# Rotary queries and keys of a hybrid layer: one product of 512 columns in place of two of 256

## The chip, the cores and the metric

The program runs on one core of a Trainium2 chip, in one launch. The metric is the device time of an execution in microseconds (us), the median of several runs. The core's engines are TensorE (PE in the rows, with its weight loads as PEld), VectorE (DVE), ScalarE (ACT), GpSimd (POOL) and SyncE (SP, which issues the DMAs here). Sums of products land in PSUM, a small memory that DVE and ACT read out ("evacuate"); everything else on the chip lies in SBUF.

## The reference, cut to what matters

Two layers over 256 tokens of width 2048. The even layer projects the normed input by one wide matrix and cuts the result up; two of the pieces, `rq` and `rk` (1024 columns each, eight heads of 128), are turned by the rotary angles and feed a retention.

```python
h = rms_norm(x, norm_g) @ w_in                       # 256 x 2048 @ 2048 x 7704
rq, rk, rv, rz, nq, kc, vc, ks, vs, kw, vw, ng, nz = split_cols(h, EVEN_SPLITS)
o = retention_chunkwise(rotary(heads(rq, 8), pos), rotary(heads(rk, 8), pos), heads(rv, 8))
...
def rotary(t, pos):
    t1, t2 = tf[..., :64], tf[..., 64:]
    return concatenate([t1 * cos - t2 * sin, t2 * cos + t1 * sin], axis=-1)
```

All is in float32. The kernel gets there by writing each factor of a projection as a high part in a shorter format (fp32r) and the rest: x = xh + xl, w = wh + wl, and the sum xh·wh + xh·wl + xl·wh. So each 128x128 block of weights costs three products.

## The kernel before

The program is a long row of projections. Each one streams its weights from HBM in pieces of 512 KB (128 partitions x 1024 numbers, tile `raw`, lines 100 to 103), ACT copies a piece to its high part (`wh`, L109), DVE subtracts to get the low part (`wl`, L110), and PE takes the products (`project`, L114). Five buffers of each of the three tiles let the loads run ahead. `prep` (L90) has a high priority in the list scheduler, which writes down a fixed order for every engine before the program runs; each engine then works through its own list in that order and waits at the head of it.

Most projections have the input as the stationary factor and 512 columns of weights as the moving one (L145 to L147; 512 columns of output, tokens on partitions). The four projections for the rotary queries and keys are flipped (`flip=True`, called at L680): 128 columns of the weights are stationary and the 256 tokens move, so that the output comes out turned, a head's 128 numbers on partitions and the tokens along a row. These are lines L139 to L141, each on 256 columns. A flipped projection is 512 columns of weights, four heads, in two PSUM tiles (`mm`, three buffers in all) with two heads in each.

When a tile is full, `evac_rotary` (L633) reads it: ACT copies the two halves of the partitions crosswise into `rot` (L640, L641), DVE multiplies the tile by the cosines into `T` (L642), and POOL multiplies `rot` by the sines and adds it (L643, L644). The cosines and sines are first multiplied by the tokens' norms (`rrow`, made by PE and copied by ACT at L235; POOL, L630 and L631, in the tile `pb`).

Between the chunks of a projection, pieces of other work are called (`extra=take(...)`). In the rotary stage these are the eight heads of the selected and windowed attention, `nsa_piece` (L604). A head is: six score products (L550 to L552, three of 512 columns and three of 256) into the PSUM tile `sc`, of which there is one buffer; four steps on DVE that add the mask, write `p` and take the row maximum (L560, with a short read of the maximum behind each); the exponentials on ACT (L567); a scaling on DVE (L574); six transposes on PE (L579); and the split of these by ACT and DVE (L459, L460). Before the first heads, DVE and ACT also write a table `pst` from the compressed attention's probabilities (`pch`, `pcl`; L538, copies of 32 partitions).

```python
        sc = ps.tile([128, 1024], F32, name="sc", tag="sc")
...
            project(ew[4 + 3 * hf + i], 512, lhs, evac_rotary(T), extra=take((1,3)), flip=True)
```

Of the kernel before, what the change touches and what calls it, by code (L numbers as in the profile page):

```python
# [13 lines left out]
F32 = mybir.dt.float32  # L14
# [8 lines left out]
S = 256  # L23
# [11 lines left out]
MMB = 3  # L35
# [6 lines left out]
           (0, 512), (1024, 1536), (2048, 2560), (512, 1024), (1536, 2048), (2560, 3072),  # L42
           (6680, 7192), (7192, 7704), (3072, 3584), (3584, 4096)]
EV_NARROW = (6656, 6680, 4096, 4608)
# [15 lines left out]
def hybrid_kernel(ctx: ExitStack, tc: tile.TileContext, a: dict, out: bass.AP):  # L60
# [53 lines left out]
    def project(src, n, lhs, evac, korder=None, lazy=None, extra=None, cut=None,  # L114
                flip=False):

        nch = src.shape[0]
        acc = [ps.tile([128, 512], F32, name=f"mm{t}", tag="mm", bufs=MMB) for t in range(2)]  # L120
        order = korder or list(range(nch))
        for i, c in enumerate(order):
            if lazy:
                lazy(c)
            parts = prep(src[c], n, cut=(lambda k: cut(c, k)) if cut and i < 3 else None)
            xh, xl = lhs[c]
            for hf in range(2):
                wh, wl = parts[hf]
                for t in range(2):
                    for j in range(2):  # L130
                        for k in range(2):
                            kk = 2 * hf + k
                            first = i == 0 and kk == 0
                            last = i == nch - 1 and kk == 3
                            if flip:
                                cs = slice((2 * t + j) * 128, (2 * t + j) * 128 + 128)
                                o = acc[t][:, j * S:j * S + S]
                                kw = dict(skip_group_check=True)
                                nc.tensor.matmul(o, wh[:, k, cs], xh[:, kk, :], start=first and j == 0, stop=False, **kw)  # L139
                                nc.tensor.matmul(o, wl[:, k, cs], xh[:, kk, :], start=False, stop=False, **kw)  # L140
                                nc.tensor.matmul(o, wh[:, k, cs], xl[:, kk, :], start=False, stop=last, **kw)  # L141
                            elif j == 0:
                                ts = slice(t * 128, t * 128 + 128)
                                o = acc[t][:, :n]
                                nc.tensor.matmul(o, xh[:, kk, ts], wh[:, k, :n], start=first, stop=False)  # L145
                                nc.tensor.matmul(o, xh[:, kk, ts], wl[:, k, :n], start=False, stop=False)  # L146
                                nc.tensor.matmul(o, xl[:, kk, ts], wh[:, k, :n], start=False, stop=last)  # L147
                    if i == nch - 1 and hf == 1:
                        with tc.high_priority(offset=HPO):
                            evac(t, acc[t])  # L150
            for f in (extra or {}).get(i, ()):
                f()
# [28 lines left out]

    def norm_block(b, gain, first=False):

        xh = xtp.tile([128, 4, S], F32R, name="xh", tag="xh")
        xl = xtp.tile([128, 4, S], F32R, name="xl", tag="xl")
# [8 lines left out]
        return xh, xl  # L194
# [51 lines left out]
    def project_both(srcs, accs, evacs):  # L246

        nch = srcs[0].shape[0]
        for c in range(nch):
            for q in range(2):  # L250
# [10 lines left out]
                xh, xl = lhs[c]  # L261
# [371 lines left out]
    def evac_rotary(T):  # L633
        rot = hp.tile([128, 4, S], F32, name="rot", tag="h")

        def f(b, p):
            hs = slice(2 * b, 2 * b + 2)
            pv = p.rearrange("p (h s) -> p h s", h=2)
            cb, sb = (x.unsqueeze(1).to_broadcast([128, 2, S]) for x in (cosR, sinR))
            nc.scalar.copy(rot[0:64, hs, :], pv[64:128])  # L640
            nc.scalar.copy(rot[64:128, hs, :], pv[0:64])  # L641
            nc.vector.tensor_tensor(T[:, hs, :], pv, cb, op=ALU.mult)  # L642
            nc.gpsimd.tensor_tensor(rot[:, hs, :], rot[:, hs, :], sb, op=ALU.mult)  # L643
            nc.gpsimd.tensor_add(T[:, hs, :], T[:, hs, :], rot[:, hs, :])  # L644
        return f
# [29 lines left out]
    for hf in range(2):  # L675
        qk = []
        for i in range(2):
            T = hp.tile([128, 4, S], F32, name=f"rT{i}_{hf}", tag="h")
            qk.append(T)
            project(ew[4 + 3 * hf + i], 512, lhs, evac_rotary(T), extra=take((1,3)), flip=True)  # L680
        v = htile(f"rv{hf}")
        project(ew[6 + 3 * hf], 512, lhs, evac_to(v), extra=take((1,3)))
# [8 lines left out]
    def mix_block(src):  # L691

        xh = xtp.tile([128, 4, S], F32R, name="xh", tag="xh")
        xl = xtp.tile([128, 4, S], F32R, name="xl", tag="xl")
# [5 lines left out]
        return xh, xl  # L700

    def gated(src, dst, r, extra):
# [3 lines left out]
        xh = xtp.tile([128, 4, S], F32R, name="xh", tag="xh")  # L706
        xl = xtp.tile([128, 4, S], F32R, name="xl", tag="xl")
# [11 lines left out]
        return (xh, xl), turn  # L719
# [6 lines left out]
    for i in range(2):  # L726
        block, turn = gated(ew[10 + i], no[i], rstd[0], first(turn, take(range(4))))
        mix.append(block)
    for i in range(2):
# [5 lines left out]
        project(ew[12 + i], 512, lhs, evac_z, extra=first(turn, take(range(4))))  # L735
# [17 lines left out]
    def turned_block(n):  # L753

        xh = xtp.tile([128, 4, S], F32R, name="xh", tag="xh")
        xl = xtp.tile([128, 4, S], F32R, name="xl", tag="xl")
# [9 lines left out]
        nxt.append((xh, xl))  # L766
# [294 lines left out]
```

## Time and profile before

| | |
|---|---|
| median of 3 runs | 939.23 us (939.16 to 939.35) |
| the profiled execution, device time | 939.11 us |
| its span (first to last instruction) | 937.3 us |
| PE busy | 930.5 us, 99% of the span |
| PEld, DVE, ACT, POOL busy | 798.7, 642.3, 507.5, 71.1 us |
| read from HBM | 170.5 MB, 184 GB/s over the span |
| the rotary stage, with the eight attention heads in it | about 133 to 275 us of the span |

A busy time is the union of an engine's instructions; matmuls overlap in the record (a matmul is shown until its results are out), so a step of PE is read from one start to the next, not from the duration. The granted clock is the share of PE's full clock (2.4 GHz) that it was given; 0.5 is 1.2 GHz. A number in brackets after a row of the timeline is the idle time of the engine before it, and what ended it.

### The profile page before, as it was taken

The page shows a single profiled execution, that of the slowest core. Times are in us where ns is not written, and L with a number is a line of the kernel's source. Part 1 is how long each engine was busy: PE and PEld are TensorE (multiplying, and loading weights), DVE is VectorE, ACT ScalarE, POOL GpSimd, SP SyncE. Part 2 cuts the span into 40 slices and gives each one's busy share as a digit, 9 for nine tenths or more (in the row PEclk, how much of TensorE's full clock was granted, in tenths as well). Part 3 has the DMA queues.
Part 4 walks back from the last instruction along what each step waited for, and adds up shares of the span by engine and source line. Part 5 has one row for each costly group of instructions (what it writes and reads, how often), then busy time and mean ns, then how long its engine had stood idle before and what let it go on. Part 6 is the DMA issues. An engine that isn't in the chain of part 4 may idle for free.

```text
span 937.3 us, 13151 instructions
## 1 busy us (share of the span) xinstructions
PE 930.5 (99%) x4949; PEld 798.7 (85%) x4949; DVE 642.3 (69%) x947; ACT 507.5 (54%) x762; POOL 71.1 (8%) x72
## 2 busy tenths in 40 slices
PE   8999999999999999999999999999999999999998
PEld 7889989989998888888888888888888888888886
DVE  7687657875654564654464499999999998546552
ACT  7566656655544544544465353556665444797341
POOL 0111100320220100000000000000000002200000
PEclk9999999999999999999999999999999999999999
DMA  9967754354446555555555555555555656434461
GB/s 332 348 204 220 249 189 149 120 176 156 152 164 207 161 170 182 185 195 181 196 185 168 192 180 180 190 190 190 185 186 185 202 197 189 148 116 157 149 226 53
DMA packets 52512, 173.48 MB, mean 185 GB/s; under 512 B 5728, under 2 KB 10720, under 8 KB 52320
## 3 DMA queue, kind: packets, MB, share of 16 engines
q1 hardware_dynamic: 52304, 172.63, 55.8%
q8 instruction: 39, 0.64, 0.3%
q14 instruction: 25, 0.20, 0.1%
q10 hardware_dynamic: 144, 0.01, 0.0%
HBM read 170.52 MB, written 2.10 MB: 184 GB/s over the span
## 4 chain that ended last, share of the span: by engine, by line
PE 97%; DMA 1%; DVE 1%; ACT 0%; issue 0%; SPq 0%; DVEq 0%
PE mm L145 25%; PE mm L147 25%; PE mm L146 25%; PE mm L139 3%; PE mm L141 3%; PE mm L140 3%; PE tr L315 3%; DMA raw<-in_ew 1%; PE dpo L931 1%; PE dsc L911 1%; PE cmph L377 1%; PE tr L579 1%; PE both L273 1%; PE both L274 0%; PE both L272 0%; PE mm L274 0%
## 5 line engine op out<-in xcount | busy, mean ns | idle before, releaser
L110 DVE TENSOR_TENSOR wl<-raw,wh 128x1024 fp32r<-128x1024 f32 (+2 forms) x322 | 385.1, 1202 | 215.0 <-ACT wh L109 208.1
L109 ACT CAST wh<-raw 128x1024 fp32r<-128x1024 f32 (+2 forms) x322 | 328.4, 1025 | 343.5 <-PE mm L147 252.1
L146 PE MATMUL mm<-wl,xh 128*128 128x512 f32 (+1 forms) x1056 | 406.4, 385 | 0.0
L145 PE MATMUL mm<-wh,xh 128*128 128x512 f32 (+1 forms) x1056 | 406.1, 386 | 0.0
L147 PE MATMUL mm<-wh,xl 128*128 128x512 f32 (+1 forms) x1056 | 403.3, 384 | 0.0
L147 PEld LDWEIGHTS mm<-wh,xl 128*128 128x128 f32 x1056 | 198.4, 188 | 38.1
L145 PEld LDWEIGHTS mm<-wh,xh 128*128 128x128 f32 x1056 | 198.2, 188 | 37.9 <-issue 0.2
L146 PEld LDWEIGHTS mm<-wl,xh 128*128 128x128 f32 x1056 | 198.5, 188 | 37.4
L801 DVE SCALAR_TENSOR_TENSOR cps<-apad,pb,cps 128x256 f32<-128x256 f32 x240 | 116.8, 487 | 5.3
L139 PE MATMUL mm<-xh,wh 128*128 128x256 f32 x256 | 73.2, 287 | 0.0
L140 PE MATMUL mm<-xh,wl 128*128 128x256 f32 x256 | 72.8, 285 | 0.0
L141 PE MATMUL mm<-xl,wh 128*128 128x256 f32 x256 | 72.5, 283 | 0.0
L140 PEld LDWEIGHTS mm<-xh,wl 128*128 128x128 f32 x256 | 49.0, 192 | 0.0
L141 PEld LDWEIGHTS mm<-xl,wh 128*128 128x128 f32 x256 | 49.0, 191 | 0.0
L139 PEld LDWEIGHTS mm<-xh,wh 128*128 128x128 f32 x256 | 48.9, 191 | 0.0
L567 ACT ACTIVATE p<-p,nm 128x128 f32<-128x128 f32 (+1 forms) x32 | 14.2, 445 | 15.5 <-DVE nm L563 15.4
L643 POOL TENSOR_TENSOR rot<-rot,pb 128x512 f32<-128x512 f32 x8 | 11.2, 1406 | 78.3 <-ACT rot L641 78.0
L299 ACT ACTIVATE sq<-d 128x128 f32<-128x128 f32 x48 | 14.3, 303 | 0.3
L273 PE MATMUL both<-wl,xh 128*128 128x512 f32 x32 | 12.8, 401 | 1.2 <-DVE wl L110 1.2
L644 POOL TENSOR_TENSOR rT<-rT,rot 128x512 f32<-128x512 f32 x8 | 13.1, 1660 | 0.0
L272 PE MATMUL both<-wh,xh 128*128 128x512 f32 x32 | 12.6, 394 | 0.0
L274 PE MATMUL both<-wh,xl 128*128 128x512 f32 x32 | 12.5, 390 | 0.0
(294 smaller groups left out, 724.0 us busy)
## 6 DMA issues: line engine op xcount, KB each, us to landing
raw<-in_ow SPq DMA_DIRECT2D x128, 512.0 KB, 4.5
raw<-in_ew SPq DMA_DIRECT2D x110, 512.0 KB, 4.2
raw<-in_ewo SPq DMA_DIRECT2D x32, 512.0 KB, 4.0
raw<-in_owo SPq DMA_DIRECT2D x24, 512.0 KB, 4.1
raw<-in_ewn SPq DMA_DIRECT2D x16, 268.0 KB, 3.5
xtok<-in_xtok SPq DMA_DIRECT2D x1, 2048.0 KB, 8.3
raw<-in_w1k SPq DMA_DIRECT2D x4, 512.0 KB, 6.4
raw<-in_w1v SPq DMA_DIRECT2D x4, 512.0 KB, 4.2
```

The costliest lines, as they stand in the source:

```text
L109: nc.scalar.copy(wh[:, k, :n], r)
L110: nc.vector.tensor_sub(wl[:, k, :n], r, wh[:, k, :n].bitcast(F32))
L139: nc.tensor.matmul(o, wh[:, k, cs], xh[:, kk, :], start=first and j == 0, stop=False, **kw)
L140: nc.tensor.matmul(o, wl[:, k, cs], xh[:, kk, :], start=False, stop=False, **kw)
L141: nc.tensor.matmul(o, wh[:, k, cs], xl[:, kk, :], start=False, stop=last, **kw)
L145: nc.tensor.matmul(o, xh[:, kk, ts], wh[:, k, :n], start=first, stop=False)
L146: nc.tensor.matmul(o, xh[:, kk, ts], wl[:, k, :n], start=False, stop=False)
L147: nc.tensor.matmul(o, xl[:, kk, ts], wh[:, k, :n], start=False, stop=last)
L273: nc.tensor.matmul(o, xh[:, kk, ts], wl[:, k, :], start=False, stop=False)
L299: nc.scalar.activation(sqv[:, t, h, :], view[:, t, h, :], AF.Square, accum_out=ss[:, t * nh + h:t * nh + h + 1])
L315: nc.tensor.transpose(pt[:, i * 128:(i + 1) * 128], b, ident)
L801: nc.vector.scalar_tensor_tensor(p, src, w, p, op0=ALU.mult, op1=ALU.add)
```

## The change

The high and the low part of a block of the input now lie in one tile `xx` (`block_pair`), so that one product with `wh` stationary can take both as one moving factor of 512 columns: `both[:, :, k, :]` is 256 columns of xh and, 1024 numbers further on, 256 of xl. Its output fills a whole PSUM tile, the left half xh·wh, the right half xl·wh; the product with `wl` (256 columns) adds to the left half. A PSUM tile now holds one head where it held two, so the four flipped projections become eight of 256 columns of weights, each with two tiles and four chunks. The weights of these come from a new input `ewt` in the same 512 KB pieces, now four blocks of 256 columns. The evacuation adds the halves first: ACT copies the right half out, DVE adds the left half to it, and the rest works from that tile `rx` in SBUF, per head in place of per pair.

```diff
+    def project_turned(src, lhs, evac, extra=None):
+        nch = src.shape[0]
+        acc = [ps.tile([128, 512], F32, name=f"mm{t}", tag="mm", bufs=MMB) for t in range(2)]
+        for c in range(nch):
+            with tc.high_priority(offset=HPO):
...
+                nc.sync.dma_start(raw, src[c])
+                nc.scalar.copy(wh, raw)
+                nc.vector.tensor_sub(wl, raw, wh.bitcast(F32))
+            xh, _, both = lhs[c]
+            for t in range(2):
+                cs = slice(t * 128, t * 128 + 128)
+                for k in range(4):
+                    last = c == nch - 1 and k == 3
+                    kw = dict(skip_group_check=True)
+                    nc.tensor.matmul(acc[t], wh[:, k, cs], both[:, :, k, :], start=c == 0 and k == 0, stop=False, **kw)
+                    nc.tensor.matmul(acc[t][:, :S], wl[:, k, cs], xh[:, k, :], start=False, stop=last, **kw)
+                if last:
+                    with tc.high_priority(offset=HPO):
+                        evac(t, acc[t])
...
+    def block_pair():
+        x = xtp.tile([128, 2, 4, S], F32R, name="xx", tag="xx")
+        return x[:, 0], x[:, 1], x
...
-        def f(b, p):
-            hs = slice(2 * b, 2 * b + 2)
-            pv = p.rearrange("p (h s) -> p h s", h=2)
-            cb, sb = (x.unsqueeze(1).to_broadcast([128, 2, S]) for x in (cosR, sinR))
-            nc.scalar.copy(rot[0:64, hs, :], pv[64:128])
-            nc.scalar.copy(rot[64:128, hs, :], pv[0:64])
-            nc.vector.tensor_tensor(T[:, hs, :], pv, cb, op=ALU.mult)
-            nc.gpsimd.tensor_tensor(rot[:, hs, :], rot[:, hs, :], sb, op=ALU.mult)
-            nc.gpsimd.tensor_add(T[:, hs, :], T[:, hs, :], rot[:, hs, :])
+        def f(h, p):
+            x = sp.tile([128, S], F32, name="rx", tag="rx", bufs=2)
+            nc.scalar.copy(x, p[:, S:])
+            nc.vector.tensor_add(x, p[:, :S], x)
+            nc.scalar.copy(rot[0:64, h, :], x[64:128])
+            nc.scalar.copy(rot[64:128, h, :], x[0:64])
+            nc.vector.tensor_mul(T[:, h, :], x, cosR)
+            nc.gpsimd.tensor_mul(rot[:, h, :], rot[:, h, :], sinR)
+            nc.gpsimd.tensor_add(T[:, h, :], T[:, h, :], rot[:, h, :])
...
-            project(ew[4 + 3 * hf + i], 512, lhs, evac_rotary(T), extra=take((1,3)), flip=True)
+            f = evac_rotary(T)
+            for j in range(2):
+                project_turned(a["ewt"][4 * hf + 2 * i + j], lhs, lambda t, p: f(2 * j + t, p), extra=take((3,)))
```

The scheduler writes a new order from this. Lines behind the new function stand 18 further down: the scores are L568 to L570 (before L550 to L552), the mask steps L578 (L560), the transposes L597 (L579), the `pst` copies L556 (L538). Two places are shown. A name's number is that of its tile.

PE at the scores of the attention's third head (`sc_2044` before), in the kernel before. The products around it (L139 to L141) are those of the second flipped projection.

```order
L139 MATMUL mm0_1920<-xh_341,wh_2082 128x256
L550 MATMUL sc_2044<-kh_562,qh0_1285 128x512
L551 MATMUL sc_2044<-kl_563,qh0_1285 128x512
L552 MATMUL sc_2044<-kh_562,ql0_1286 128x512
L550 MATMUL sc_2044<-kh_562,qh0_1285 128x256
L551 MATMUL sc_2044<-kl_563,qh0_1285 128x256
L552 MATMUL sc_2044<-kh_562,ql0_1286 128x256
L140 MATMUL mm0_1920<-xh_341,wl_2083 128x256
L141 MATMUL mm0_1920<-xl_342,wh_2082 128x256
```

The same place on PE in the changed kernel; the third head's scores are `sc_1984`, the fourth's `sc_2127`.

```order
L570 MATMUL sc_1984<-kh_558,ql0_1282 128x512
L568 MATMUL sc_1984<-kh_558,qh0_1281 128x256
L569 MATMUL sc_1984<-kl_559,qh0_1281 128x256
L570 MATMUL sc_1984<-kh_558,ql0_1282 128x256
L568 MATMUL sc_2127<-kh_558,qh0_1281 128x512
L569 MATMUL sc_2127<-kl_559,qh0_1281 128x512
L570 MATMUL sc_2127<-kh_558,ql0_1282 128x512
L568 MATMUL sc_2127<-kh_558,qh0_1281 128x256
L569 MATMUL sc_2127<-kl_559,qh0_1281 128x256
L570 MATMUL sc_2127<-kh_558,ql0_1282 128x256
L160 MATMUL mm1_1877<-xx_163,wh_1879 128x512
L161 MATMUL mm1_1877<-xx_163,wl_1880 128x256
```

Before, projection work follows the third head's scores, and the fourth head's stand 143 products of projections further on. Now the fourth head's follow at once, and just ahead of the third's stand the six transposes of the first head. The other heads' scores have projection work behind them in both kernels.

DVE from the last mask step of the second head (`sc_1859`) to the third head's, in the kernel before:

```order
L560 ISA p_1867,nm_1866<-sc_1859,pm_518 128x2x128
L560 ISA nm_1866 128x1
L110 TENSOR_TENSOR wl_2083<-raw_2081,wh_2082 128x1024
L460 TENSOR_TENSOR pTl_1691<-tr_1717,pTh_1690 128x4x128
L563 TENSOR_SCALAR nm_1866<-nm_1866 128x4
L642 TENSOR_TENSOR rT0_0_1565<-mm0_1567,pb_521 128x512
L642 TENSOR_TENSOR rT0_0_1565<-mm1_1568,pb_521 128x512
L460 TENSOR_TENSOR pTl_1691<-tr_1724,pTh_1690 128x2x128
L560 ISA p_2052,nm_2051<-sc_2044,pm_518 128x128
L560 ISA nm_2051 128x1
L560 ISA p_2052,nm_2051<-sc_2044,pm_518 128x2x128
L560 ISA nm_2051 128x1
```

The same stretch of DVE in the changed kernel (the second head's scores are `sc_1815`):

```order
L578 ISA p_1823,nm_1822<-sc_1815,pm_514 128x2x128
L578 ISA nm_1822 128x1
L556 COPY pst0_1526<-pcl_1518 32x256 x4
L556 COPY pst1_1527<-pcl_1518 32x256 x4
L581 TENSOR_SCALAR nm_1822<-nm_1822 128x4
L660 TENSOR_TENSOR rT0_0_1561<-rx_1645,pb_517 128x256
L660 TENSOR_TENSOR rT0_0_1561<-rx_1661,pb_517 128x256
L478 TENSOR_TENSOR pTl_1671<-tr_1697,pTh_1670 128x4x128
L478 TENSOR_TENSOR pTl_1671<-tr_1704,pTh_1670 128x2x128
L578 ISA p_1992,nm_1991<-sc_1984,pm_514 128x128
L578 ISA nm_1991 128x1
L578 ISA p_1992,nm_1991<-sc_1984,pm_514 128x2x128
```

The eight copies of `pcl`, which stood among the second head's mask steps, now stand between the second head's and the third's, as do the two cosine products; the subtraction L110 has moved ahead. Two more mask steps of the third head follow.

## Rows read from the trace of the kernel before

**Rows 1.** The page, the chain that ended last: shares of the span by engine.

```profile
PE 97%; DMA 1%; DVE 1%; ACT 0%; issue 0%; SPq 0%; DVEq 0%
```

**Rows 2.** Groups by form, 131 to 277 us: shapes xcount | busy us, mean ns | idle.

```profile
L139 PE MATMUL mm<-xh,wh 128*128 128x256 f32 x256 | 73.2, 287 | 0.0
```

**Rows 3.** Timeline of PE, flipped products: start us, us, what.

```profile
133.85 0.28 PE L139 MATMUL mm<-xh,wh 128*128 128x256 f32 x1
...
142.48 0.28 PE L139 MATMUL mm<-xh,wh 128*128 128x256 f32 x1
```

**Rows 4.** The chain in order of time, an ordinary projection: start us, us.

```profile
124.84 0.23 PE mm L147
...
131.64 0.23 PE mm L147
```

**Rows 5.** Timeline of PE, one head's scores among flipped products.

```profile
153.26 0.39 PE L552 MATMUL sc<-kh,ql 128*128 128x512 f32 x1
153.49 0.28 PE L550 MATMUL sc<-kh,qh 128*128 128x256 f32 x1
153.60 0.28 PE L551 MATMUL sc<-kl,qh 128*128 128x256 f32 x1
```

**Rows 6.** Busy time by stretch: us, PE, PEld, DVE, ACT, POOL, PEclk, DMA share, GB/s.

```profile
155.00:177.00 22.00, 22.00 (x179) 21.60 (x178) 20.02 (x66) 16.84 (x45) 7.37 (x6) 1.00 0.25 84
```

**Rows 7.** Timeline of PE, scores of the third head and of the fourth.

```profile
168.62 0.40 PE L550 MATMUL sc<-kh,qh 128*128 128x512 f32 x1
...
169.67 0.28 PE L140 MATMUL mm<-xh,wl 128*128 128x256 f32 x1
...
190.61 0.40 PE L550 MATMUL sc<-kh,qh 128*128 128x512 f32 x1
```

**Rows 8.** Timeline of DVE, 150 to 173 us.

```profile
150.92 0.42 DVE L520 TENSOR_TENSOR pc<-pc,cm 128x256 f32<-128x256 f32 x1
...
155.60 0.16 DVE L563 TENSOR_SCALAR nm<-nm 128x4 f32<-128x4 f32 x1
...
163.98 2.39 DVE L538 CAST pst<-pcl 32x256 fp32r<-32x256 f32 x8
...
167.28 1.65 DVE L110 TENSOR_TENSOR wl<-raw,wh 128x1024 fp32r<-128x1024 f32 x1
168.85 0.68 DVE L460 TENSOR_TENSOR pTl<-tr,pTh 128x512 fp32r<-128x512 f32 x1
169.45 0.65 DVE L563 TENSOR_SCALAR nm<-nm 128x4 f32<-128x4 f32 x1
...
171.21 0.41 DVE L460 TENSOR_TENSOR pTl<-tr,pTh 128x256 fp32r<-128x256 f32 x1
171.54 0.28 DVE L560 CUSTOM_DVE_ANT_0 p<-sc,pm 128x128 f32<-128x128 f32 x1
...
172.30 0.41 DVE L560 CUSTOM_DVE_ANT_0 p<-sc,pm 128x256 f32<-128x256 f32 x1
```

**Rows 9.** Timeline of POOL, the same stretch.

```profile
166.40 0.75 POOL L630 TENSOR_TENSOR pb<-pb,rrow 128x256 f32<-128x256 f32 x1 [28.22 <-ACT rrow L235]
...
167.92 3.42 POOL L643 TENSOR_TENSOR rot<-rot,pb 128x512 f32<-128x512 f32 x2
```

**Rows 10.** Timeline of ACT, the same stretch.

```profile
164.40 0.58 ACT L641 COPY rot<-mm 64x512 f32<-64x512 f32 x1
...
165.96 0.36 ACT L235 COPY rrow<-tr 128x256 f32<-128x256 f32 x1
```

**Rows 11.** Timeline, the last product of PE.

```profile
933.11 0.39 PE L147 MATMUL mm<-wh,xl 128*128 128x512 f32 x1
```

**Rows 12.** Busy time by stretch behind the last product; columns as rows 6.

```profile
935.00:936.00 1.00, 0.00 (x0) 0.00 (x0) 0.00 (x0) 0.00 (x0) 0.00 (x0) 0.81 0.61 208
```

**Rows 13.** Timeline of PE, the warming products at the start, in two cuts.

```profile
0.97 2.74 PE L165 MATMUL cold<-heat 128*128 128x128 bf16 x24 [0.97 <-DVE heat L162]
...
3.72 0.87 PE L165 MATMUL cold<-heat 128*128 128x128 bf16 x12
```

More of the change, by code (lines that the diff above doesn't have):

```diff
@@ L112, in prep, with project @@
         return parts
-    def project(src, n, lhs, evac, korder=None, lazy=None, extra=None, cut=None,
-                flip=False):
+    def project(src, n, lhs, evac, extra=None):
         nch = src.shape[0]
         acc = [ps.tile([128, 512], F32, name=f"mm{t}", tag="mm", bufs=MMB) for t in range(2)]
[L121 to L126, printed above, removed]
+        for c in range(nch):
+            parts = prep(src[c], n)
+            xh, xl, _ = lhs[c]
             for hf in range(2):
@@ L129, in project @@
                 for t in range(2):
[L130 to L147, printed above, removed]
@@ L148, in project @@
-                    if i == nch - 1 and hf == 1:
+                    ts = slice(t * 128, t * 128 + 128)
+                    o = acc[t][:, :n]
+                    for k in range(2):
+                        kk = 2 * hf + k
+                        last = c == nch - 1 and kk == 3
+                        nc.tensor.matmul(o, xh[:, kk, ts], wh[:, k, :n], start=c == 0 and kk == 0, stop=False)
+                        nc.tensor.matmul(o, xh[:, kk, ts], wl[:, k, :n], start=False, stop=False)
+                        nc.tensor.matmul(o, xl[:, kk, ts], wh[:, k, :n], start=False, stop=last)
@@ L149, in project @@
+                    if last:
                         with tc.high_priority(offset=HPO):
                             evac(t, acc[t])
-            for f in (extra or {}).get(i, ()):
+            for f in (extra or {}).get(c, ()):
+                f()
+    def project_turned(src, lhs, evac, extra=None):
+        nch = src.shape[0]
+        acc = [ps.tile([128, 512], F32, name=f"mm{t}", tag="mm", bufs=MMB) for t in range(2)]
+        for c in range(nch):
+            with tc.high_priority(offset=HPO):
+                raw, wh, wl = (wp.tile([128, 2, 512], d, name=n, tag=n).rearrange("p a (b n) -> p (a b) n", n=256)
+                               for n, d in (("raw", F32), ("wh", F32R), ("wl", F32R)))
+                nc.sync.dma_start(raw, src[c])
[9 more added lines that the diff above has]
+                    nc.tensor.matmul(acc[t][:, :S], wl[:, k, cs], xh[:, k, :], start=False, stop=last, **kw)
+                if last:
+                    with tc.high_priority(offset=HPO):
+                        evac(t, acc[t])
+            for f in (extra or {}).get(c, ()):
@@ L691, in mix_block @@
     def mix_block(src):
-        xh = xtp.tile([128, 4, S], F32R, name="xh", tag="xh")
-        xl = xtp.tile([128, 4, S], F32R, name="xl", tag="xl")
+        xh, xl, xx = block_pair()
         for j in range(2):
@@ L726, in hybrid_kernel @@
     for i in range(2):
-        block, turn = gated(ew[10 + i], no[i], rstd[0], first(turn, take(range(4))))
+        block, turn = gated(ew[6 + i], no[i], rstd[0], first(turn, take(range(4))))
         mix.append(block)
@@ L734, in evac_z @@
             nc.vector.tensor_mul(o[:, t, :], o[:, t, :], z[:, t, :])
-        project(ew[12 + i], 512, lhs, evac_z, extra=first(turn, take(range(4))))
+        project(ew[8 + i], 512, lhs, evac_z, extra=first(turn, take(range(4))))
         turn = lambda i=i: mix.append(mix_block(ros[i]))
@@ L753, in turned_block @@
     def turned_block(n):
-        xh = xtp.tile([128, 4, S], F32R, name="xh", tag="xh")
-        xl = xtp.tile([128, 4, S], F32R, name="xl", tag="xl")
+        xh, xl, xx = block_pair()
         for j in range(2):
```

23 lines of the change are left out of this document (12 added, 11 removed).

## The prediction, made before the changed kernel ran

> **What bounds the kernel now.** I began with the chain that ended last [rows 1]: 97% of it is PE. So the time is the sum of PE's steps, and any other engine matters only where PE stands still for it. In the rotary stage PE does not: the stretch from 155 to 177 us has PE busy for all of its 22.00 us at the full clock, although DVE is busy for 20.02 of them [rows 6]. That pair of numbers is the thing to keep: PE is the bound, DVE is the next one by a small margin, and only the order in which things stand keeps DVE's lateness from PE.
>
> A busy time says nothing of a PE step here, because the records overlap (287 ns shown for a product of 256 columns [rows 2]). I took steps from start to start. Flipped products: from 133.85 to 142.48 us there are 24 triples, 72 steps, so 8.63 / 72 = 0.120 us each [rows 3]. Ordinary products of 512 columns: from 124.84 to 131.64 us there are 30 steps, 6.80 / 30 = 0.227 us [rows 4]. Twice the columns cost 0.107 us more, not 0.120: each product has some 13 ns that do not grow with its columns. Among the scores, where the two sizes stand side by side, the steps are again 0.23 behind a 512 and 0.11 to 0.12 behind a 256 [rows 5], so mixing them costs nothing.
>
> **The change, part by part.**
>
> *Products.* There are 256 triples, 256 products on each of the three lines [rows 2]. A triple costs 3 x 0.120 = 0.360 us before and 0.227 + 0.120 = 0.347 us after: 0.013 us x 256 = **3.3 us saved**, all on PE, all on the path. The columns are the same, 768 a triple; only one product in three goes. What weighs against even this is the Trainium skill. Its page "TensorE: Matmul & The Clock Gate", section "Back-to-back issue gap", gives a product's fixed share at full clock as 2.5 ns; by that an estimate of the saving is 0.6 us, and the sum below would end 2.7 us higher. The rows above disagree with it (13 ns), and the rows decide.
>
> *Loads and splits.* The rotary weights come in 32 pieces of 512 KB before and after, and ACT and DVE split each the same way: nothing. Laying xh and xl in one tile moves no work: nothing.
>
> *Evacuation.* Per head ACT gets a copy of 256 columns out of PSUM, priced at 0.36 us by the copy at L235 [rows 10], and two crosswise copies at half the width of those that take 0.58 us [rows 10]; DVE gets an addition of 256 columns, 0.42 us by its nearest row, L520 [rows 8]. Sixteen heads: about 7 us more on DVE over 140 us of stage. The next projection starts in the third buffer, and PE needs the first tile of a projection back only when the next one's second tile begins, sixteen products or 8 x 0.347 = 2.8 us after it was full; I cost this at nothing by itself. The cover is PE's own work, and if it goes, each late addition would cost about its 0.42 us.
>
> *The fourth head's scores.* This is the part that decides. In the new order they stand directly behind the third head's. There is one buffer of `sc`, so PE must stop until DVE has done the third head's four mask steps, and PE's list offers nothing else meanwhile. Before, the third head's scores began at 168.62 us and the fourth's only at 190.61 [rows 7], with products of projections between, so that DVE's lateness (last mask step of the third head ending 172.30 + 0.41 = 172.71 us [rows 8]) cost nothing.
>
> How long does it stop? PE can start the third head's scores when DVE is through with the second's; they take 169.67 - 168.62 = 1.05 us [rows 7]. In DVE's list between the two heads' last mask steps there now stand: eight copies for `pst`, 2.39 us; one small scaling L563, 0.16 us undisturbed; two cosine products of 256 columns, 2 x 0.42 us by L520; two splits, 0.68 + 0.41 us; the third head's four mask steps, 172.71 - 171.54 = 1.17 us [rows 8]. Sum: 2.39 + 0.16 + 0.84 + 1.09 + 1.17 = 5.65 us.
>
> POOL lengthens this. Beside POOL's L643 the small scaling took 0.65 us in place of 0.16, and the split L110 took 1.65 us [rows 8, 9]: an instruction of DVE that reads SBUF waits until POOL's is out. POOL now has four instructions there (two of 0.75 us by L630 [rows 9], two of about that), just when DVE copies. Bounds: nothing, or all four in turn, 2.9 us. I take 0.6 us, one or two such waits as seen. The Trainium skill's page "SBUF — State Buffer", section "Who interferes with whom", says that copies in particular can take the port pair that DVE shares with GpSimd, as an exclusive lock; no row of this trace has a DVE copy beside POOL. By it an estimate would lie near the upper bound, and the sum 2 us higher.
>
> So PE stands for 5.65 + 0.6 - 1.05 = **5.2 us**. It could be a microsecond less if PE comes late to the third head's scores (ahead of them are six transposes, whose PSUM tile ACT must empty first with L235 [rows 10]), so 3.6 us at the low end; 7.5 us with all of POOL's turns.
>
> *The clock.* A stop of that length has no equal inside this trace, but the end of it shows what follows one. The last product ended at 933.11 + 0.39 = 933.50 us [rows 11]; the granted clock has a mean of 0.81 from 935 to 936 us [rows 12], which is full until 935.62 and half behind it. So the clock fell 2.1 us after the last product, and a stop of 5.2 us should take it to 1.2 GHz. Back up: the warming products at the start step by (2.74 - 0.31) / 23 = 0.106 us until about 3.8 us and half that later [rows 13] (0.31 us is one of them at that clock), so the clock rose 2.8 us after the first. If PE runs 2.8 us at half clock behind the stop, half of it is lost: **1.4 us**. Ends: nothing, if the clock stays; 2.8 us, if the rise takes twice as long.
>
> **The sum**, against the profiled execution's 939.11 us (its span is 937.3 us, 1.8 us lie around it): 939.11 - 3.3 + 5.2 + 1.4 = 942.4 us. The median of the runs is 0.1 us above that execution, so **942.5 us**, 0.35% slower.
>
> **The rivals.**
>
> *The wait, without the clock* (17 in 100). As above, but the clock stays at full through the stop: 942.5 - 1.4 = 941.1 us. For it: the only fall seen is behind the very last product. Against: 2.1 us sufficed there, less than half of this stop.
>
> *No wait worth the name* (14 in 100): the kernel ends on the other side, 939.2 - 3.3 = 935.9 us. The mechanism is that PE comes to the scores later than DVE does to their masks, say because transposes or an accumulator hold PE earlier in places that cost nothing extra, or because DVE, with fewer splits in the way, has caught up. It decides from a wait under 1.4 us (3.3 less the 1.9 us of 0.2%). Against it: the scores themselves need 1.05 us and the mask steps another 1.17 behind them, and DVE is busy for nine tenths of this stretch [rows 6].
>
> *The products save nothing* (6 in 100), with the wait and the clock as forecast: the long product, whose moving factor lies in two stretches, steps at 2 x 0.120 us like the two that it replaces. 942.5 + 3.3 = 945.8 us. For it: no product of the trace moves two separate stretches of that size. Against: rows 5. The page on TensorE named above would put a case between, at 2.7 us over the forecast, by its smaller fixed share.
>
> The forecast itself has what is left, 63 in 100.
>
> **How the numbers follow.** 0.2% is 1.9 us, about what a measurement of this kernel can tell from no change: faster means below 937.4, slower above 941.1 us. Faster is the second rival, 0.14. The first rival sits on the upper bound, so half of it is "same"; with 3 in 100 of the forecast, where the stop is at its shortest and the clock hardly falls, "same" has 0.11. The rest, 0.75, is slower. The forecast's own range runs from a stop of 3.6 us with 0.7 us of clock (940.2) to one of 6.6 us with 2.8 us (945.3). To hold 8 in 10 I take in the first rival and leave out the second and most of the third: 939.8 to 945.2 us.
>
> **What would show it.** In the profile of the changed kernel: 256 products of 512 columns stepping at 0.227 us and 256 of 256 columns at 0.120; PE, without a pause in this stretch now [rows 6], with one wait of 4 to 7 us at the fourth head's first score (L568), released by DVE's mask step L578; a granted clock under 1.00 in the stretch behind it, and steps of about twice the length there for some 3 us; no new wait elsewhere. The prediction is wrong if that wait is under 2 us, if PE waits instead for an accumulator (a wait at L160 released by DVE's addition L657), or if the long product steps at 0.24 us.

## The result, and the profile after

The changed kernel takes 944.43 us (median of 4 runs, 943.72 to 944.97) beside 939.19 us for the kernel before on the same chip (4 runs, 938.79 to 939.35). The ratio is 1.0056, with a 95% interval of 1.0044 to 1.0068: slower by 5.2 us. The forecast was 942.5 us, in a range from 939.8 to 945.2.

The page of the changed kernel, its span, its engines and the chain that ended last:

```profile
span 942.4 us, 12722 instructions
PE 930.7 (99%) x4693; PEld 787.1 (84%) x4693; DVE 648.6 (69%) x971; ACT 517.1 (55%) x794; POOL 72.5 (8%) x88
...
PE 97%; DVE 2%; DMA 1%; ACT 0%; SPq 0%; issue 0%; DVEq 0%
```

PE still makes up 97% of this chain, but DVE has gone from 1% [rows 1] to 2%. One per cent of 942 us is large enough to hold the whole loss, so the question is where DVE got onto the path. The chain's shares by line name `pst` L556, the copies of the compressed weights.

PE's timeline in the changed kernel answers it. Columns: start us, us, engine, line, operation; in brackets the idle time before the row and what ended it.

```profile
133.63 0.40 PE L160 MATMUL mm<-xx,wh 128*128 128x512 f32 x1
...
142.99 0.40 PE L160 MATMUL mm<-xx,wh 128*128 128x512 f32 x1
...
167.49 0.48 PE L568 MATMUL sc<-kh,qh 128*128 128x512 f32 x1
...
168.50 0.28 PE L570 MATMUL sc<-kh,ql 128*128 128x256 f32 x1
174.39 0.76 PE L568 MATMUL sc<-kh,qh 128*128 128x512 f32 x1 [5.61 <-DVE nm L578]
174.96 0.63 PE L569 MATMUL sc<-kl,qh 128*128 128x512 f32 x1
...
176.45 0.63 PE L160 MATMUL mm<-xx,wh 128*128 128x512 f32 x1
176.88 0.41 PE L161 MATMUL mm<-xx,wl 128*128 128x256 f32 x1
177.09 0.63 PE L160 MATMUL mm<-xx,wh 128*128 128x512 f32 x1
...
179.01 0.44 PE L160 MATMUL mm<-xx,wh 128*128 128x512 f32 x1
179.29 0.28 PE L161 MATMUL mm<-xx,wl 128*128 128x256 f32 x1
...
183.19 0.40 PE L160 MATMUL mm<-xx,wh 128*128 128x512 f32 x1
...
186.72 0.40 PE L160 MATMUL mm<-xx,wh 128*128 128x512 f32 x1
```

Three things are to be read here. First the stop: the last product of the third head's scores starts at 168.50 us and the fourth's first at 174.39, 5.89 us where a step is 0.12, so the stop costs 5.8 us. DVE's mask step L578 ends it. Second, the steps behind it are too long: 0.43 us from 176.45 to 176.88 and 0.21 from there to 177.09, about twice the usual. From 174.39 to 179.01 us PE does six score products and four pairs, which at full clock take 3 x 0.227 + 3 x 0.120 + 4 x 0.347 = 2.43 us; they take 4.62, so 2.2 us are lost. Third, the pairs: 27 of them from 133.63 to 142.99 us step by 0.347 us, ten from 183.19 to 186.72 by 0.353. Over the stage the median is 0.35 us against 0.36 for a triple before (its first steps are in [rows 3]), so 256 pairs save about 2.6 us.

Busy time by stretch in the changed kernel (us, PE, PEld, DVE, ACT, POOL, PEclk, DMA share, GB/s), the first row to be laid beside [rows 6]:

```profile
155.00:177.00 22.00, 16.39 (x91) 14.22 (x90) 20.78 (x70) 15.05 (x43) 5.85 (x8) 0.89 0.26 90
172.00:173.00 1.00, 0.00 (x0) 0.00 (x0) 1.00 (x3) 1.00 (x6) 0.96 (x2) 0.64 0.00 0
174.00:175.00 1.00, 0.61 (x2) 0.55 (x3) 1.00 (x7) 0.38 (x1) 0.00 (x0) 0.50 0.00 0
...
178.00:179.00 1.00, 1.00 (x4) 0.81 (x4) 1.00 (x3) 0.45 (x2) 0.52 (x1) 0.50 0.00 0
179.00:180.00 1.00, 1.00 (x7) 0.87 (x7) 0.93 (x6) 0.97 (x1) 0.00 (x0) 0.95 0.00 0
```

PE's 22.00 busy us of before are 16.39 here, while DVE's 20.02 are 20.78: the engine that had been late all along is now waited for. The mean of 0.64 from 172 to 173 us puts the fall to 1.2 GHz at 172.28, 3.5 us after PE's last product; the mean of 0.95 puts the rise at 179.1, 4.7 us after PE went on. (A stretch that is partly at 0.5 and partly at 1.00 gives its turning point by its mean.)

What DVE did meanwhile, from its timeline in the changed kernel (to be read with [rows 8]):

```profile
166.80 0.42 DVE L578 CUSTOM_DVE_ANT_0 p<-sc,pm 128x256 f32<-128x256 f32 x1
167.15 0.09 DVE L578 DVE_READ_ACCUMULATOR2_ANT nm<- 128x1 f32 x1
167.26 4.08 DVE L556 CAST pst<-pcl 32x256 fp32r<-32x256 f32 x8
171.38 0.17 DVE L581 TENSOR_SCALAR nm<-nm 128x4 f32<-128x4 f32 x1
171.46 0.75 DVE L660 TENSOR_TENSOR rT<-rx,pb 128x256 f32<-128x256 f32 x2
172.13 1.01 DVE L478 TENSOR_TENSOR pTl<-tr,pTh 128x512 fp32r<-128x512 f32 x2
173.06 0.28 DVE L578 CUSTOM_DVE_ANT_0 p<-sc,pm 128x128 f32<-128x128 f32 x1
...
174.16 0.08 DVE L578 DVE_READ_ACCUMULATOR2_ANT nm<- 128x1 f32 x1
```

The first four of the eight copies, one by one:

```profile
167.26 0.61 DVE L556 CAST pst<-pcl 32x256 fp32r<-32x256 f32 x1
167.88 0.74 DVE L556 CAST pst<-pcl 32x256 fp32r<-32x256 f32 x1
168.63 0.79 DVE L556 CAST pst<-pcl 32x256 fp32r<-32x256 f32 x1
169.44 0.72 DVE L556 CAST pst<-pcl 32x256 fp32r<-32x256 f32 x1
```

And POOL's timeline in the same stretch [rows 9]:

```profile
167.00 0.73 POOL L648 TENSOR_TENSOR pb<-pb,rrow 128x256 f32<-128x256 f32 x1 [29.02 <-ACT rrow L253]
167.69 0.79 POOL L649 TENSOR_TENSOR pb<-pb,rrow 128x256 f32<-128x256 f32 x1
168.55 1.46 POOL L661 TENSOR_TENSOR rot<-rot,pb 128x256 f32<-128x256 f32 x2
172.04 1.43 POOL L662 TENSOR_TENSOR rT<-rT,rot 128x256 f32<-128x256 f32 x2 [2.04 <-DVE rT L660]
```

From the second head's last mask step to the third's DVE has no pause: 174.24 - 167.24 = 7.0 us. The eight copies, 2.39 us before [rows 8], take 4.08. POOL's first four instructions (L648, L649 and two of L661) run until 170.01 us, and each of the first four copies ends about 0.15 us after one of them is out; the last four, with POOL idle, take 0.28 or 0.29 us each.

The balance by this trace is - 2.6 + 5.8 + 2.2 = + 5.4 us, against 5.2 measured. What it leaves open is what the wait hangs on: the place of the scores in PE's list, POOL, or all that DVE has to do there.

### The profile page after: what moved, and what is told of

Read it like the earlier page. It is cut to its first block, busy times and chain, and to the rows that moved or that the text cites. A ratio compares the mean times of both kernels' runs of the same rounds, so it can differ in the third digit from the quotient of the medians.

```text
span 942.4 us, 12722 instructions
## 1 busy us (share of the span) xinstructions
PE 930.7 (99%) x4693; PEld 787.1 (84%) x4693; DVE 648.6 (69%) x971; ACT 517.1 (55%) x794; POOL 72.5 (8%) x88
## 4 chain that ended last, share of the span: by engine, by line
PE 97%; DVE 2%; DMA 1%; ACT 0%; SPq 0%; issue 0%; DVEq 0%
PE mm L133 25%; PE mm L135 25%; PE mm L134 25%; PE mm L160 6%; PE mm L161 3%; PE tr L333 2%; PE dpo L948 1%; PE dsc L928 1%; PE cmph L395 1%; PE both L291 1%; PE both L292 1%; PE both L290 1%; DVE pst L556 1%; PE mm L292 1%; PE mm L291 1%; PE mm L290 1%
## 5 line engine op out<-in xcount | busy, mean ns | idle before, releaser
L113 DVE TENSOR_TENSOR wl<-raw,wh 128x1024 fp32r<-128x1024 f32 (+2 forms) x290 | 344.8, 1195 | 192.4 <-ACT wh L112 185.7
L134 PE MATMUL mm<-wl,xx 128*128 128x512 f32 (+1 forms) x1056 | 406.4, 385 | 0.0
L133 PE MATMUL mm<-wh,xx 128*128 128x512 f32 (+1 forms) x1056 | 406.2, 386 | 0.0
L135 PE MATMUL mm<-wh,xx 128*128 128x512 f32 (+1 forms) x1056 | 403.1, 384 | 0.0
L135 PEld LDWEIGHTS mm<-wh,xx 128*128 128x128 f32 x1056 | 198.4, 188 | 38.1
L133 PEld LDWEIGHTS mm<-wh,xx 128*128 128x128 f32 x1056 | 198.3, 188 | 38.1 <-issue 0.2
L134 PEld LDWEIGHTS mm<-wl,xx 128*128 128x128 f32 x1056 | 198.5, 188 | 37.4
L160 PE MATMUL mm<-xx,wh 128*128 128x512 f32 x256 | 92.1, 401 | 0.0
L161 PE MATMUL mm<-xx,wl 128*128 128x256 f32 x256 | 72.4, 284 | 0.0
L160 PEld LDWEIGHTS mm<-xx,wh 128*128 128x128 f32 x256 | 48.6, 191 | 10.3
L153 DVE TENSOR_TENSOR wl<-raw,wh 128x1024 fp32r<-128x1024 f32 x32 | 39.3, 1230 | 19.4 <-ACT wh L152 19.4
L161 PEld LDWEIGHTS mm<-xx,wl 128*128 128x128 f32 x256 | 48.9, 191 | 0.3
L661 POOL TENSOR_TENSOR rot<-rot,pb 128x256 f32<-128x256 f32 x16 | 12.3, 774 | 89.8 <-ACT rot L659 82.2
L662 POOL TENSOR_TENSOR rT<-rT,rot 128x256 f32<-128x256 f32 x16 | 12.8, 812 | 2.7 <-DVE rT L660 2.0
L578 DVE CUSTOM_DVE_ANT_0 p<-sc,pm 128x128 f32<-128x128 f32 (+1 forms) x32 | 9.8, 354 | 4.4 <-PE sc L570 4.4
```

The source lines that it names most:

```text
L113: nc.vector.tensor_sub(wl[:, k, :n], r, wh[:, k, :n].bitcast(F32))
L133: nc.tensor.matmul(o, xh[:, kk, ts], wh[:, k, :n], start=c == 0 and kk == 0, stop=False)
L153: nc.vector.tensor_sub(wl, raw, wh.bitcast(F32))
L160: nc.tensor.matmul(acc[t], wh[:, k, cs], both[:, :, k, :], start=c == 0 and k == 0, stop=False, **kw)
L161: nc.tensor.matmul(acc[t][:, :S], wl[:, k, cs], xh[:, k, :], start=False, stop=last, **kw)
```

## The experiments

All were run beside the kernel before, whose medians were 938.96 us beside e1 to e4, 939.04 beside e5 to e8 and 939.02 beside e9; these three groups ran on three chips.

**e1_unadjacent: the fourth head's scores held back.**

```diff
+    done = []
...
+                    if last:
+                        done.append(m.ins)
...
-        for t, o in ((1, sc[:, :512]), (0, sc[:, 512:768])):
+        with tc.issue_after(done[5]) if h == 3 else ExitStack():
+            for t, o in ((1, sc[:, :512]), (0, sc[:, 512:768])):
```

> The fourth head's scores are held back until the last product of the third half projection, so that they no longer stand behind the third head's scores in PE's list; nothing else is edited. Theory A (the neighbourhood in PE's list is the cause): the wait of 5.6 us and the stretch at half clock (2.25 us) go, 944.4 - 5.8 - 2.25 = about 936.4 us. Theory B (VectorE's backlog is the cause: eight copies of the compressed weights, mask steps and splits stand there in one piece, and the addition that empties the accumulators stands behind the third head's mask steps): TensorE then goes on to the next half projection and stops there instead, at its first product for an accumulator that has not been emptied, for 5 to 6.5 us, and the clock falls as before: 943 to 945.5 us. I hold B the likelier, 70 to 30.

Measured: 944.09 us (943.86 to 945.83, 5 runs; ratio 1.0059, 1.0046 to 1.0071), no better than the change. PE's timeline (lines 2 and more further down, L162 is the pair's first product, L662 the addition at the evacuation) has the same stop at another door:

```profile
174.26 0.79 PE L162 MATMUL mm<-xx,wh 128*128 128x512 f32 x1 [5.82 <-DVE rx L662]
```

Theory B holds. The scores' neighbourhood, on which the forecast rested, isn't needed: the loss stays without it. With the scores out of the way PE goes on with a product for an accumulator, and that is emptied by an addition that stands behind the same mask steps in DVE's list. The forecast had priced a late addition at nothing, or at 0.42 us if its cover went.

**e2_row_early: GpSimd's multiplications by the norms taken out of the place.**

```diff
+    rrow = token_row(rstd[0], "rrow")
+    cosR = small["cosT"]
+    sinR = small["sinT"]
+    nc.gpsimd.tensor_mul(cosR, cosR, rrow)
+    nc.gpsimd.tensor_mul(sinR, sinR, rrow)
     gates = const.tile([128, 2, 24], F32, name="gates")
...
-    rrow = token_row(rstd[0], "rrow")
...
```

> The row of reciprocal norms and its two GpSimd multiplications (cosine and sine) are written ahead of the gates' projection, so GpSimd does them before the heads begin; the eight copies of the low weights then no longer run beside them. Theory A (contention of the copies with GpSimd is what made the wait longer than forecast): the copies take 2.4 us as before the change and not 4.1, the wait is 3.9 us, the time 942.7 us, or 940.5 if the clock no longer falls. Theory B (VectorE's backlog as a whole, the rest of GpSimd's rotary work moves into the place): a wait of 5 to 5.6 us stays on one of the heads' scores, the clock falls, 943 to 944.4 us.

Measured: 942.91 us (942.46 to 944.23, 5 runs; ratio 1.0046, 1.0033 to 1.0058). On DVE's timeline the eight low copies, with POOL idle beside them, and ahead of them four copies of the high part, which now run beside POOL's rotary work (L661 and L662, 164.91 to 168.27 us):

```profile
166.23 2.49 DVE L561 CAST pst<-pch 32x256 fp32r<-32x256 f32 x4
...
169.61 2.38 DVE L561 CAST pst<-pcl 32x256 fp32r<-32x256 f32 x8
```

And the stop on PE's timeline, now at the third head's first score and ended by the second head's mask:

```profile
172.58 0.77 PE L573 MATMUL sc<-kh,qh 128*128 128x512 f32 x1 [4.91 <-DVE nm L583]
```

The low copies bear out A's first half: 2.38 us alone and 4.08 beside POOL, for the same eight instructions. But the contention has moved and not gone: four copies that would take half of 2.38 us alone take 2.49 beside POOL. The median time, 942.91 us, lies between the theories' times (942.7; 943 to 944.4) and doesn't decide. The wait speaks for B: it is 0.7 us shorter and not 1.7. The scheduler's new order also puts the copies ahead of the second head's last mask step and the stop ahead of the third head. So contention is a part of the backlog; what the wait would be with none of it, this run does not show. Three executions had a mean granted clock of 0.998 (942.46 to 942.91 us) and two 0.996 (943.87 and 944.23, the latter the profiled one), a first sign of what the half clock is worth.

**e3_copies_act: the copies with their head, and on ScalarE.**

```diff
-    for h in range(8):
+    def spread(h):
...
-            (nc.vector.tensor_copy if n else nc.scalar.copy)(pst[g][32 * n:32 * n + 32, h % 4], v)
+            nc.scalar.copy(pst[g][32 * n:32 * n + 32, h % 4], v)
...
             nsa_head(h, npt["h"], npt["l"])
+            spread(h)
```

> The copies of the compressed weights are written with the head that they belong to, and all done by ScalarE: 16 copies leave VectorE's list before the fourth head. Theory (VectorE's backlog sets the wait): 2.4 to 4 us less of work ahead of the mask steps, the wait falls to 2 to 3.5 us; in so short a stop the clock should hold (it fell 3.5 us after the last product began to end). 944.4 - 2.6 - 2.25 = 939.6 us, 938.5 to 940.5. If the clock falls in the shorter stop too, 941 to 942. If the copies were not what the mask steps waited for, 944.4.

Measured: 940.86 us (939.11 to 941.24, 11 runs; ratio 1.0018, 1.0009 to 1.0027). PE's timeline:

```profile
168.30 0.28 PE L570 MATMUL sc<-kh,ql 128*128 128x256 f32 x1
171.33 0.47 PE L568 MATMUL sc<-kh,qh 128*128 128x512 f32 x1 [2.75 <-DVE nm L578]
171.64 0.51 PE L569 MATMUL sc<-kl,qh 128*128 128x512 f32 x1
171.95 0.63 PE L570 MATMUL sc<-kh,ql 128*128 128x512 f32 x1
```

Its busy time by stretch, columns as above:

```profile
171.00:172.00 1.00, 0.67 (x3) 0.55 (x4) 0.93 (x5) 0.96 (x4) 0.00 (x0) 0.88 0.00 0
...
174.00:175.00 1.00, 1.00 (x5) 0.82 (x4) 0.03 (x1) 0.98 (x6) 0.00 (x0) 0.50 0.00 0
175.00:176.00 1.00, 1.00 (x7) 0.88 (x7) 0.93 (x5) 0.96 (x3) 0.15 (x1) 0.91 0.00 0
```

The wait fell by 2.9 us, inside the bounds given, with the fourth head's scores still directly behind the third's; so DVE's backlog sets it. I had expected the clock to hold in so short a stop, and it did not: it fell at 171.76 us by the mean of 0.88, when PE had already gone on. One execution of the eleven tells more than the others: its mean granted clock was 1.000 and it took 939.11 us, where the ten at 0.997 or 0.998 took 940.56 to 941.24. Kernel and order are the same, so this is what the half clock is worth, 1.4 to 2.1 us, unless that execution's stop was shorter too, which its record does not tell.

**e4_both: the two easings together.** Its edit is e2's and e3's.

> Both of the former: the row early, and the copies late and on ScalarE. If VectorE's backlog is the whole cause, at most 1 us of waiting is left and the clock holds: 944.4 - 5.8 - 2.25 + 1 = 937.4 us, 936.2 to 938; that is before's 939.2 less what the products save (2.6 us) plus what is left of the wait. If smaller evacuations or the finer half projections cost time of their own, it stays above 939.

Measured: 937.39 us (937.09 to 937.83, 11 runs; ratio 0.9984, 0.9975 to 0.9993): faster than the kernel before. Its mean granted clock is 0.999 or 1.000 in every execution. All that is left of the stop, on PE's timeline and on DVE's:

```profile
169.73 0.49 PE L160 MATMUL mm<-xx,wh 128*128 128x512 f32 x1 [0.80 <-DVE rx L658]
...
169.25 0.76 DVE L658 TENSOR_TENSOR rx<-mm,rx 128x256 f32<-128x256 f32 x2 [3.37 <-ACT rx L657]
```

DVE isn't late here any more: it stood idle for 3.37 us until ACT's copy L657 came, and that stands in ACT's list behind twelve of the copies that were moved there (4.97 us in one piece).

And its busy time from 155 to 177 us:

```profile
155.00:177.00 22.00, 21.20 (x127) 18.44 (x126) 17.18 (x55) 19.25 (x52) 6.47 (x8) 1.00 0.27 94
```

DVE has 17.18 us to do there in place of 20.78, ACT 19.25 in place of 15.05, and PE is back at 21.20 of 22. The whole loss is undone by moving work that isn't PE's; the products stay as changed. The scheduler's order has changed as well: projection work now follows the third head's scores. So it is e3, and not e4, that eases DVE with the neighbourhood kept.

**e5_three and e6_before_eased: what the products are worth.** e5 is e4 with the products alone undone; e6 is the kernel before with e4's easing.

```diff
-                    nc.tensor.matmul(acc[t], wh[:, k, cs], both[:, :, k, :], start=c == 0 and k == 0, stop=False, **kw)
+                    nc.tensor.matmul(acc[t][:, :S], wh[:, k, cs], xh[:, k, :], start=c == 0 and k == 0, stop=False, **kw)
                     nc.tensor.matmul(acc[t][:, :S], wl[:, k, cs], xh[:, k, :], start=False, stop=last, **kw)
+                    nc.tensor.matmul(acc[t][:, S:], wh[:, k, cs], both[:, 1, k, :], start=False, stop=last, **kw)
```

> The former kernel (row early, copies late and on ScalarE) with the products alone undone: three products of 256 columns for each triple, the third one into the accumulator's upper half, so that loads, splits, half projections and the addition at the evacuation stay as they are. Theory (the products save 10 ns a pair against a triple, 2.6 us in all, and the former kernel gives 0.95 us of it back in one wait at its accumulators): 937.4 + 2.6 - 0.95 = 939.0 us, 938.6 to 939.6. Rival 1 (the products save the 3.3 us that I forecast): 939.8. Rival 2 (what is faster there are the eased heads, not the products): 937.4 or less.

> The kernel before the change with the same easing alone: row early, copies with their head and on ScalarE. It has no half projections, no addition at the evacuation and three products a triple. Theory (before has hardly a wait at the heads to ease: 0.3 us in all from 140 to 215 us): 938.6 to 939.1 us, within 0.4 of before and of the former kernel with three products, so that the finer half projections and the addition cost nothing by themselves. Rival (easing is what gained): about 937.4, and the changed products have no part in it.

Measured: e5 939.62 us (939.10 to 940.58, 11 runs; ratio 1.0008, 0.9999 to 1.0016), e6 938.72 us (938.24 to 940.42, 11 runs; ratio 0.9999, 0.9990 to 1.0007). Easing does nothing for the kernel before, so what it gives the changed kernel is the removal of its own wait. Between e4 and e5, on two chips, lie 2.2 us. Each keeps a short wait: e4's step to 169.73 us is 0.95 us too long, and e5 has two steps at transposes (L603, released by DVE) that are 0.74 us too long together. Without these the products are worth 2.2 + 0.95 - 0.74 = 2.4 us, near the 2.6 of the steps. The theory's number for e5 was 0.6 us low (its range ended at 939.6), since it did not reckon with waits in e5 too; rival 1 isn't excluded by the median alone (939.8), but the steps exclude it. The finer half projections by themselves come to 939.62 - 0.74 - 938.72, 0.2 us, which cannot be told from nothing here.

**e7_filled: products of zeros in the stop.** `m` is the last score product.

```diff
+        if h == 2:
+            with tc.issue_after(m.ins):
+                for i in range(60):
+                    nc.tensor.matmul(sc[:, 768:896], heat, heat, start=True, stop=True)
```

> Sixty products of 128 columns of bf16 zeros (56 to 65 ns each, 3.4 to 3.9 us) are issued behind the third head's scores, into unused columns; they compute nothing. They keep TensorE at work in the stretch where it stood still. With them there, the fourth head's scores come later in PE's list, and by the rows of the neighbourhood the product for the accumulator then waits for 1.5 to 2.5 us of VectorE's backlog. Theory (the half clock is a term of its own, paid because TensorE stood still): no half clock, about 944.4 - 2.25 = 942.2 us, 941.5 to 942.6. Rival (the clock falls whatever TensorE does there, or costs nothing beside the wait): 944 to 944.5.

Measured: 942.33 us (942.18 to 943.95, 5 runs; ratio 1.0044, 1.0030 to 1.0058). PE's timeline:

```profile
168.74 3.13 PE L574 MATMUL sc<-heat 128*128 128x128 bf16 x53
173.81 0.50 PE L160 MATMUL mm<-xx,wh 128*128 128x512 f32 x1 [1.94 <-DVE rx L661]
174.15 0.28 PE L161 MATMUL mm<-xx,wl 128*128 128x256 f32 x1
174.28 0.39 PE L160 MATMUL mm<-xx,wh 128*128 128x512 f32 x1
...
180.22 0.56 PE L574 MATMUL sc<-heat 128*128 128x128 bf16 x7
```

From 168 to 174 us its granted clock:

```profile
168.00:174.00 6.00, 4.06 (x60) 3.75 (x59) 5.71 (x15) 2.85 (x12) 3.44 (x5) 1.00 0.00 0
```

DVE is nearly as late as before: PE resumes real work 173.81 - 168.74 = 5.1 us behind the scores. But the clock is full, the steps behind it are 0.34 and 0.13 us, and 2.1 us come back against 944.43. Not all of that is the clock: the stop is 0.7 us shorter than the 5.8 of the changed kernel, since the scheduler also moved the fourth head's scores and DVE's order, and seven of the sixty products stand further on among useful ones, where they cost about 0.4 us. That leaves 2.1 - 0.7 + 0.4 = 1.8 us for the clock, near the 2.2 read above. Work that computes nothing made the kernel faster, which speaks for the half clock as a cost of its own. Two of the five executions had a mean clock of 0.998 and took 943.46 and 943.95 us against 942.18 to 942.33 for the three at 1.000, 1.1 to 1.8 us for the clock once more, with the order the same; where in these two the clock fell is not on record.

**e8_longer: all copies on VectorE.**

```diff
-            (nc.vector.tensor_copy if n else nc.scalar.copy)(pst[g][32 * n:32 * n + 32, h % 4], v)
+            nc.vector.tensor_copy(pst[g][32 * n:32 * n + 32, h % 4], v)
```

> The changed kernel with the eight copies that ScalarE made done by VectorE too: 2.4 us more of its work alone, up to 4.1 beside GpSimd, ahead of the third head's mask steps, and more behind it. Theory (the wait is VectorE's backlog and grows with it one for one, while the half clock costs the same): 4 to 5.5 us on top, 948.4 to 950 us, the wait 9.6 to 11.5 us. Rival (the wait has another end, ScalarE's or GpSimd's work): under 1 us more, 944.4 to 945.4.

Measured: 945.89 us (945.65 to 946.23, 4 runs; ratio 1.0075, 1.0062 to 1.0089). PE's timeline:

```profile
174.93 0.77 PE L568 MATMUL sc<-kh,qh 128*128 128x512 f32 x1 [7.35 <-DVE nm L578]
```

The size was missed by more than 2 us, the direction was right: the wait grew by 7.35 - 5.61 = 1.7 us, the time by 1.5. The scheduler put the second head's mask steps behind nearly all copies, so it is the third head's scores that wait here, from 167.6 us on; the stop ends only 0.5 us later than in the changed kernel, with one head's scores less done. That a longer list on DVE lengthens the wait, and the time with it, is shown; that it does so one for one with the copies is not.

**e9_third_buffer: one more `rx`.**

```diff
-            x = sp.tile([128, S], F32, name="rx", tag="rx", bufs=2)
+            x = sp.tile([128, S], F32, name="rx", tag="rx", bufs=3)
```

> The fastest kernel so far (row early, copies late and on ScalarE) with a third buffer for the emptied half accumulator (rx, bufs 2 to 3); nothing else is edited. What is left there is one wait of 0.95 us of a half projection's first product, for an accumulator that VectorE's addition had not emptied. Theory (that addition stands late because both rx buffers were still being read): the wait goes, 936.4 us, 936.1 to 936.8. Rival (the addition stands late because of the mask steps ahead of it in VectorE's list, or the wait comes back at a later accumulator): 937.1 to 937.6, no change.

Measured: 937.05 us (936.73 to 937.76, 11 runs; ratio 0.9979, 0.9969 to 0.9988), between theory and rival. The wait of 0.80 us is gone. A smaller one has come up on PE's timeline, at a weight split in the next projection:

```profile
197.06 0.50 PE L134 MATMUL mm<-wl,xx 128*128 128x512 f32 x1 [0.29 <-DVE wl L113]
```

Its gain over e4 (0.3 us) is within what the two ranges leave open. Neither theory nor rival named what e4's row shows, that the addition waited for ACT's copy; with three buffers, three heads' `rx` are read ahead of the moved copies in ACT's list, where it was two. It is the fastest version found, 2.0 us under the kernel before beside it and 7.4 under the change as made.

## Why the prediction was right, and where it was off

*Sign, place and order of size:* right. The change gains on PE and loses more to one stop in which PE waits for DVE's mask steps of the third head; no other new wait of that size is in the trace. The likeliest case was the one that came.

*Products, 3.3 us:* too high by about a quarter. The step that failed is the term 0.227 + 0.120 us for a pair. That holds in the first half projection (0.347), but over the stage the median pair takes 0.35 us and the median triple 0.36, so a product less saves some 10 ns and not 13: about 2.6 us by the steps, 2.4 by e4 against e5. The rival that the products save nothing falls. So does the estimate of 0.6 us worked out from the 2.5 ns in the Trainium skill's page "TensorE: Matmul & The Clock Gate", section "Back-to-back issue gap", which gives it for a matmul by itself: a product less saves four times that here.

*Loads, splits, evacuation at nothing:* right in the sum (0.2 us by e5 and e6, within the noise), but for a reason that hid something. The forecast gave each late addition a price of 0.42 us if its cover went. e1 shows what it can really cost: the addition stands in DVE's list behind the same backlog, so the accumulator was a second door at which PE would have stopped for 5.8 us.

*The wait, 5.2 us:* 5.8 measured, inside the bounds of 3.6 to 7.5. The mis-sized part is POOL. I took 0.6 us for it, one or two of its turns; the copies alone grew by 4.08 - 2.38 = 1.7 us beside it. All four turns came, as in the forecast's upper bound, and lasted 2.9 us (167.26 to 170.16); but the four copies would have taken 1.2 of these anyway. The Trainium skill's page "SBUF — State Buffer", section "Who interferes with whom", had said that copies can take the port pair shared with GpSimd, as an exclusive lock: the copies of the changed kernel, each out just after an instruction of POOL, agree with that, and so does e2 (2.49 us for four in place of 1.19). The forecast's sentence that an instruction of DVE that reads SBUF waits for POOL is too wide: the two splits L478 took 1.01 us beside POOL's L662, no longer than before the change (0.68 + 0.41, [rows 8]). In part the wait came near by luck. The POOL term was 1.1 us too small and the others about 0.5 too large: the cosine products and splits took less than their rows of before (0.75 + 1.01 us against 1.93), and PE began the third head's scores 0.25 us after DVE was through with the second's, and not at once.

The mechanism as worded, that the scores stand side by side, tells where PE stops in the changed kernel, but not why it must: e1 took the neighbourhood away and kept the wait; e3 kept the neighbourhood, took work from DVE, and the wait fell by half; in e4 all but 0.8 us of it went.

*The clock, 1.4 us:* too low, 2.2 measured, within the ends of nothing and 2.8. The clock fell as forecast, but came back 4.7 us after PE went on, not 2.8 as at the start [rows 13]: a single stretch was too little to size the term. The first rival, the wait without the clock at 941.1 us, falls by the trace.

The errors were one-sided: 0.7 us less saved, 0.6 more waiting, 0.8 more for the clock, 2.1 in all by these terms, 1.9 by the medians.

## What to carry to other kernels

When the bound engine has no pause although another is busy for nine tenths of the same stretch, look for every door at which the first could be made to wait for the second (here a score buffer and an accumulator): here moving one group of products shut one door and the stop went to the next (e1), while taking work off the late engine did away with it. The engine that gets the work can then be the late one: the 0.8 us left in e4 hung on ScalarE's list. In this kernel a saving of some nanoseconds in each of many products is real and small, and one stop of a few microseconds outweighs it, in itself and again in the half clock behind it; so a change that gains on the bound engine should be made together with the easing of the next one (here 937.4 or 937.1 us with both, 944.4 with the first alone, 938.7 with the second alone).

## What the runs showed of the hardware that I had not expected

- The half clock followed a stop of PE of 2.75 us in e3's profiled execution; the mean granted clock of ten of its eleven executions was down to 0.997 or 0.998. In the profiled executions with a stop of 1.94 us (e7) and 0.80 us (e4) it stayed at full.
- A lowered mean is not tied to such a stop alone: e6 has one execution at 0.998 of eleven (940.42 us), and the kernel before, whose profile shows no stop of 2 us behind its start, two of fifteen beside e9 (940.69 and 940.83 us against a median of 939.02). So e7's two executions at 0.998 don't show that a stop of 1.94 us lowers the clock.
- Between the end of PE's last product and the fall lay 2.1 us at the end of the kernel before [rows 11, 12], 2.7 in e1, 3.5 in the changed kernel, 4.1 in e2 and 4.8 in e8; in e3 the fall came 0.4 us after PE had gone on. So the forecast's 2.1 us was one case of a spread.
- After PE had gone on, it ran at half clock for 4.7 us in the changed kernel, and until 3.7 (e1) to 6.0 us (e2) had passed in the other stops that the clock fell in; the start of the kernel before shows 2.8 [rows 13].
- Products of 128 columns of zeros, bf16, kept the full clock through a stretch without useful work (e7).
- Eight copies of 32 partitions x 256 on DVE took 2.38 us with POOL idle (e2) and 4.08 us with POOL's multiplications beside the first four; each of these four ended about 0.15 us after one of POOL's instructions.
